# Layer-norm statistics spread by transposing a column of stride 0, and their three sums taken in one group of matmuls

## The chip, the cores and the metric

The kernel runs on one core of one Trainium2 chip. The metric is the time of one execution on the device, in microseconds (us). Times of several executions are given as a median with the lowest and the highest.

## What is computed

A two-layer backbone (a Conformer convolution layer and a bidirectional mLSTM layer, each followed by a squared-ReLU MLP) over 256 context tokens and 256 latent tokens of width 1024. Each of its sub-layers ends in a layer norm of a residual sum. The part that the change touches is the layer norm of layer 0, which runs on both streams:

```python
def layer_norm(x, g, b):
    xf = x.astype(jnp.float32)
    mu = jnp.mean(xf, axis=-1, keepdims=True)
    var = jnp.mean(jnp.square(xf - mu), axis=-1, keepdims=True)
    return ((xf - mu) * lax.rsqrt(var + LN_EPS) * g.astype(jnp.float32) + b.astype(jnp.float32)).astype(x.dtype)
...
        h = layer_norm(ALPHA * h + g1 * y, ln1_g[i], ln1_b[i])
        h = layer_norm(ALPHA * h + g2 * sq_relu_mlp(modulate(h, sh2, sc2), mlp_w1[i], mlp_w2[i]), ln2_g[i], ln2_b[i])
        if need_ctx:
            hc = layer_norm(ALPHA * hc + cg1 * yc, ln1_g[i], ln1_b[i])
            hc = layer_norm(ALPHA * hc + cg2 * sq_relu_mlp(modulate(hc, csh2, csc2), mlp_w1[i], mlp_w2[i]), ...)
```

## The kernel before

In layer 0 the residual stream `x` lies transposed: eight tiles of 128 channels (partitions) by 512 tokens, the context tokens in columns 0 to 255 (`LO`) and the latent tokens in 256 to 511 (`HI`). [...] All large products are done in three single-pass matmuls on a weight split into a high and a low part (`mm3`, lines 180, 183 and 184), each of 256 or 512 columns; ScalarE casts the high part (line 149) and VectorE subtracts it to get the low one (line 150).

The class `Norm` (from line 486) handles one norm of one half, n = 256 tokens, so nb = n/P = 2 blocks of 128 tokens. There are four of them: after the second pointwise convolution (`pw2_epi`, for LO and then HI) and after the first MLP (`feed0`, for HI and then LO). I call them norms A (LO, near 190 to 208 us), B (HI, 218 to 236 us), C (HI, 551 to 567 us) and D (LO, 577 to 597 us). Each goes through these steps:

- `add` (lines 502 and 504) sums the eight tiles on VectorE into `acc`, as they come out of the matmuls.
- `mean` (line 509), after the fourth tile: a matmul with `inv_h` (line 510) gives a provisional mean `k`, the same in every partition, and ScalarE copies it to SBUF (line 511). Then `col` takes the column `kc`, the token-wise value of `k`, from `acc` as it stands.
- `shift` (lines 525 to 531) subtracts `k` from each tile on VectorE, squares the result on ScalarE and adds the squares up in `s2` on VectorE. It is a chain of links, one for each tile.
- `finish` (line 543) takes the columns `mu` (from the complete `acc`) and `ms` (from `s2`), each by `col`; subtracts `kc` from `mu`; forms the variance, its root on ScalarE (line 557), the reciprocal (line 559) and minus mean times reciprocal (line 560). `rn` then has four columns: two of rstd, two of -mean*rstd, with one token in each partition. To use them they must be spread: each token's value has to stand in all 128 partitions, along the free axis. Before the change, VectorE multiplies four copies of the identity by the four columns (`dg`, line 566, a 128x512 tile of four diagonals), and one matmul of `ones` with `dg` (line 571) gives a PSUM bank with rstd in columns 0 to 255 and -mean*rstd in 256 to 511.
- `apply` (lines 577 and 578) multiplies and adds on VectorE, and ScalarE and VectorE turn the result into the next product's input (lines 600 and 601).

`col` (lines 534 to 541) is a group of nb = 2 one-column matmuls, `src` block as the stationary operand and `inv_c` as the moving one (line 538), and one VectorE instruction that scales them into SBUF (line 540). A matmul of two fp32 operands that is not a transpose leaves two records in the trace, each with its own weight load.

The small results lie in PSUM tiles with the tag "ln", of which two can be held at a time; the transposes of the convolution's second half (`silu`, line 975) use the same two while norm A runs. `tmp("L")`, two tiles, holds `dg`, the squares of line 530 and other temporaries.

The order of the instructions on each engine is, with few exceptions (`issue_after`, `keep_in_program_order`), not written out by hand. A planner sets it when the kernel is built: of the instructions whose inputs and tiles are ready by its own estimate of the costs, it takes the one that comes first in the program. So the matmuls of a norm stand in the middle of a run of large matmuls, at the place where the planner took their inputs to be ready. On the chip each engine keeps to that order and waits at a semaphore if the inputs are later.

Line 1808, elsewhere in the kernel, has a stationary operand of stride 0:

```python
nc.tensor.matmul(ps, fold[:, 2 * v + 1:2 * v + 2].broadcast_to([P, P]), ada_n3.sb, start=True, stop=True)
```

Of the kernel before, what the change touches and what calls it, by code (L numbers as in the profile page):

```python
# [8 lines left out]
F32 = mybir.dt.float32  # L9
# [3 lines left out]
ALU = mybir.AluOpType  # L13

P = 128
D = 1024
# [4 lines left out]
T = 512  # L21
# [4 lines left out]
L = 128  # L26
# [44 lines left out]
def hybrid_kernel(ctx: ExitStack, tc: tile.TileContext, xT, vecs_d, wdw_d, ada0_w, ada_w, wg_d, pw1a, pw1, pw2, w1_0, w2_0,  # L71
                  w1_1, w2_1, up_x, up_z, wv, wo, bo_d, wk, wq, wqT, wdown, rows_d, out):
    nc = tc.nc
    PSUM = bass.MemoryType.PSUM
    con = ctx.enter_context(tc.tile_pool(name="con", bufs=1))
# [8 lines left out]
    def nm(s):  # L84
        uid[0] += 1
        return f"{s}_{uid[0]}"
# [3 lines left out]
    def tmp(tag, dt=F32):  # L90
        return tp.tile([P, T], dt, tag=tag, name=nm(tag), bufs={"E": 4, "S": 2, "L": 2, "F": 1}[tag])
# [8 lines left out]
    def psum(tag="mm"):  # L100
        return pp.tile([P, 512], F32, tag=tag, name=nm(tag), bufs={"mm": 3, "ln": 2, "fl": 1, "cv": 2}[tag])
# [23 lines left out]
    ident = con.tile([P, P], F32, name="ident")  # L125
    make_identity(nc, ident)
    ones = con.tile([P, P], F32, name="ones")
# [2 lines left out]
    nc.vector.memset(inv_h, 1.0 / DH)  # L130
    inv_c = con.tile([P, 1], F32, name="inv_c")
    nc.vector.memset(inv_c, 1.0 / D)
    eps = con.tile([P, 1], F32, name="eps")
    nc.vector.memset(eps, EPS)

# [350 lines left out]
    class Norm:  # L486
# [21 lines left out]
        def mean(self):  # L508
            kp = psum("ln")[:, :self.n]
            nc.tensor.matmul(kp, inv_h, self.acc, start=True, stop=True)  # L510
            nc.scalar.copy(self.k, kp)
            self.kc = self.col(self.acc, 2.0 / D)

        def feed(self, t):

# [15 lines left out]
                nc.vector.tensor_tensor(self.s2, self.s2, sq, op=ALU.add)  # L531
            self.i += 1

        def col(self, src, scale):
            nb = self.n // P
            ps = psum("ln")
            for b in range(nb):
                nc.tensor.matmul(ps[:, b:b + 1], src[:, b * P:(b + 1) * P], inv_c, start=True, stop=True)
            c = con.tile([P, nb], F32, name=nm("lc"))
            nc.vector.tensor_scalar(c, ps[:, :nb], scale * D, None, op0=ALU.mult)  # L540
            return c

        def finish(self, fill=()):

            fill = list(fill)
            n, nb = self.n, self.n // P
            if fill:
                fill.pop(0)()
            mu = self.col(self.acc, 1.0 / D)
            if fill:  # L550
                fill.pop(0)()
            ms = self.col(self.s2, 1.0 / D)
            nc.vector.tensor_tensor(mu, mu, self.kc, op=ALU.subtract)
            m2 = con.tile([P, nb], F32, name=nm("lc"))
            nc.vector.tensor_tensor(m2, mu, mu, op=ALU.mult)
            nc.vector.tensor_tensor(ms, ms, m2, op=ALU.subtract)
            nc.scalar.activation(ms, ms, AF.Sqrt, bias=eps)
            rn = con.tile([P, 2 * nb], F32, name=nm("lc"))
            nc.vector.reciprocal(rn[:, :nb], ms)
            nc.vector.scalar_tensor_tensor(rn[:, nb:], mu, -1.0, rn[:, :nb], op0=ALU.mult, op1=ALU.mult)  # L560
            for f_ in fill:
                f_()
            outp = []
            for i in range(0, 2 * nb, 4):
                dg = tmp("L")
                nc.vector.tensor_tensor(
                    dg.rearrange("p (b c) -> p b c", b=4),
                    ident.rearrange("p (o c) -> p o c", o=1).broadcast_to([P, 4, P]),
                    rn[:, i:i + 4].rearrange("p (b o) -> p b o", o=1).broadcast_to([P, 4, P]), op=ALU.mult)
                ps = psum("ln")  # L570
                nc.tensor.matmul(ps, ones, dg, start=True, stop=True)
                outp += [ps[:, j:j + n] for j in range(0, T, n)]
            self.rstd, self.nmr = outp

        def apply(self, f, sl=slice(None)):
            t = self.ts[f][:, sl]
# [1269 lines left out]
    for c in range(4):  # L1846
# [40 lines left out]
        if last:  # L1887
            nc.scalar.activation(con.tile([P, 1], F32, name=nm("warm")), eps, AF.Sqrt)
            for hf in range(2):
                for kt, w in last:  # L1890
                    w2_mm(w, kt, 0, hf)
                residual(0, hf, acc[0][hf], G2)
                if hf == 0:
                    part(acc[1][1], HF[1])
            finish(0)
            for kt, w in last:
                w2_mm(w, kt, 1, 0)
            part(acc[1][0], HF[0])
            for q in range(2):
                quarter(q)  # L1900
            for q, sl in HALVES:
                ps = psum()[:, :C]
                for i, (kt, w) in enumerate(last):
                    mm3t(ps, hid[kt][0][:, BLK[1]], hid[kt][1][:, BLK[1]], w[0][1][:, sl], w[1][1][:, sl],
                         i == 0, i == len(last) - 1)
                quarter(2 + q, ps)
            finish(1)
# [79 lines left out]
```

## Time and profile before

| | |
|---|---|
| time, median of 3 (lowest to highest) | 1675.88 us (1675.58 to 1676.01) |
| time of the profiled execution | 1676.15 us |
| span of the profiled execution | 1674.3 us |
| TensorE busy | 1662.7 us, 99% of the span |
| VectorE busy | 1034.4 us, 62% |
| ScalarE busy | 742.5 us, 44% |
| mean granted TensorE clock | 0.999 |

In the profile PE stands for TensorE's matmuls and PEld for its weight loads, which overlap them; DVE is VectorE, ACT ScalarE, POOL GpSimd, SP SyncE. L571 is line 571 of the kernel. A row of a timeline has the start in us from the span's start, the time taken, the engine, the line, the operation, output and inputs, their shapes, and how many instructions in a row are merged into it. Matmuls overlap: a matmul's own time runs from its issue to its modelled end, so a busy PE isn't told from a fast one by its busy time. What a group of matmuls costs is seen by the starts of the matmuls before and behind it.

### The profile page before, as it was taken

Reading aid. Unit: us, or ns where it says so; the run is one execution under the profiler, and the core shown is the slowest. Engines: PE = TensorE matmul, PEld = TensorE weight load, DVE = VectorE, ACT = ScalarE, POOL = GpSimd, SP = SyncE. Lnnn points to the kernel's source line nnn. Section 1 sums busy time; section 2 is a strip of 40 time slices with the busy share of each in tenths; the row PEclk is TensorE's granted clock in tenths of the full one; section 3 lists DMA queues with packets and bytes.
Section 4 is the critical chain, followed back from the end, with each engine's and each line's share of the span. In section 5 each row is a group of like instructions: output and inputs, shape, how many; then the busy total and the mean of one; then the engine's idle time right before and its main releaser. Section 6 shows DMA issues by size and latency. Waiting matters only on the chain.

```text
span 1674.3 us, 22935 instructions
## 1 busy us (share of the span) xinstructions
PE 1662.7 (99%) x8944; PEld 1369.3 (82%) x8944; DVE 1034.4 (62%) x1877; ACT 742.5 (44%) x1196; POOL 14.3 (1%) x64
## 2 busy tenths in 40 slices
PE   9999999999999999999999999999999999999998
PEld 7665898888888998877788899888878888778887
DVE  6555895666645775752143653464389876786677
ACT  4312573232324466642232542442368654555453
POOL 0000000000000000000000000000000000000001
PEclk9999999999999999999999999999999999999999
DMA  9547223434424065566685753455375555675552
GB/s 356 196 153 273 86 74 114 151 126 144 145 101 151 2 202 191 175 206 248 252 270 170 249 188 120 133 207 168 134 246 187 194 213 212 245 274 188 186 182 95
DMA packets 73035, 301.61 MB, mean 180 GB/s; under 512 B 7422, under 2 KB 23586, under 8 KB 42848
## 3 DMA queue, kind: packets, MB, share of 16 engines
q1 hardware_dynamic: 55216, 285.44, 48.7%
q10 hardware_dynamic: 17712, 14.72, 2.6%
q8 instruction: 70, 1.15, 0.3%
q14 instruction: 37, 0.30, 0.1%
HBM read 284.37 MB, written 15.77 MB: 179 GB/s over the span
## 4 chain that ended last, share of the span: by engine, by line
PE 95%; DVE 2%; DMA 1%; ACT 0%; issue 0%; SPq 0%; DVEq 0%; ACTq 0%
PE mm L180 17%; PE mm L184 17%; PE mm L183 17%; PE mm L195 7%; PE mm L211 4%; PE mm L213 4%; PE mm L196 4%; PE mm L212 4%; PE cv L211 1%; PE cv L213 1%; PE cv L212 1%; PE fl L342 1%; PE ln L180 1%; PE cv L855 1%; PE fl L772 1%; PE ln L183 1%
## 5 line engine op out<-in xcount | busy, mean ns | idle before, releaser
L150 DVE TENSOR_TENSOR wl<-raw,wh 128x1024 fp32r<-128x1024 f32 x344 | 418.6, 1221 | 272.0 <-ACT wh L149 269.6
L149 ACT CAST wh<-raw 128x1024 fp32r<-128x1024 f32 x344 | 358.4, 1050 | 496.2 <-PE mm L183 271.8
L183 PE MATMUL mm<-u,wh 128*128 128x512 f32 (+1 forms) x808 | 291.9, 361 | 0.3 <-DVE u L610 0.2
L180 PE MATMUL mm<-u,wh 128*128 128x512 f32 (+1 forms) x680 | 244.5, 360 | 0.0
L184 PE MATMUL mm<-u,wl 128*128 128x512 f32 (+1 forms) x680 | 241.5, 356 | 0.0
L183 PEld LDWEIGHTS mm<-u,wh 128*128 128x128 f32 x808 | 152.7, 189 | 23.3 <-issue 1.0
L180 PEld LDWEIGHTS mm<-u,wh 128*128 128x128 f32 x680 | 128.5, 189 | 25.8 <-issue 7.2
L184 PEld LDWEIGHTS mm<-u,wl 128*128 128x128 f32 x680 | 128.4, 189 | 18.7 <-issue 1.0
L211 PE MATMUL mm<-wh,xl 128*128 128x512 f32 x256 | 101.1, 395 | 0.8 <-ACT wh L149 0.8
L180 PE MATMUL mm<-xm,wh 128*128 128x512 f32 x256 | 101.0, 395 | 0.0
L212 PE MATMUL mm<-wh,xl 128*128 128x512 f32 x256 | 100.1, 391 | 0.0
L184 PE MATMUL mm<-xm,wl 128*128 128x512 f32 x256 | 99.7, 390 | 0.0
L213 PE MATMUL mm<-wl,xl 128*128 128x512 f32 x256 | 99.4, 392 | 0.3 <-DVE wl L150 0.3
L180 PE MATMUL mm<-hid,wh 128*128 128x512 f32 (+1 forms) x256 | 93.3, 364 | 0.0
L183 PE MATMUL mm<-hid,wh 128*128 128x512 f32 (+1 forms) x256 | 92.8, 363 | 0.0
L184 PE MATMUL mm<-hid,wl 128*128 128x512 f32 (+1 forms) x256 | 92.8, 363 | 0.0
L195 PE MATMUL mm<-x,wh 128*128 128x512 f32 x232 | 81.1, 398 | 0.0
L425 DVE SCALAR_TENSOR_TENSOR S<-ar,cs,S 128x512 f32<-128x512 f32 x56 | 40.8, 750 | 62.0 <-DMA ar<-ada_w 61.6
L183 PE MATMUL mm<-qq,wh 128*128 128x272 f32 x256 | 73.9, 289 | 0.0
L180 PE MATMUL mm<-qq,wh 128*128 128x272 f32 x256 | 73.5, 288 | 0.0
L184 PE MATMUL mm<-qq,wl 128*128 128x272 f32 x256 | 73.5, 288 | 0.0
L195 PE MATMUL mm<-u,wh 128*128 128x512 f32 x192 | 68.7, 398 | 0.0
(533 smaller groups left out, 3269.7 us busy)
## 6 DMA issues: line engine op xcount, KB each, us to landing
raw<-w SPq DMA_DIRECT2D x64, 1024.0 KB, 4.8
raw<-wo SPq DMA_DIRECT2D x32, 1024.0 KB, 4.8
raw<-ada_w SPq DMA_DIRECT2D x24, 1024.0 KB, 6.4
ar<-ada_w SPq DMA_DIRECT2D x80, 256.0 KB, 3.6
raw<-wv SPq DMA_DIRECT2D x16, 1024.0 KB, 7.9
raw<-wqT SPq DMA_DIRECT2D x16, 1024.0 KB, 5.9
raw<-wq SPq DMA_DIRECT2D x16, 1024.0 KB, 5.4
raw<-wk SPq DMA_DIRECT2D x16, 1024.0 KB, 5.6
```

The source lines that it names most:

```text
L149: c = nc.scalar.copy(hi, src)
L150: lastsub[0] = nc.vector.tensor_tensor(lo, src, hi.bitcast(F32), op=ALU.subtract).ins
L180: a = nc.tensor.matmul(ps, wh, xh, start=start, stop=False)
L183: nc.tensor.matmul(ps, wh, xl, start=False, stop=False)
L184: lastmm[0] = nc.tensor.matmul(ps, wl, xh, start=False, stop=stop).ins
L195: todo = [lambda s_, e_: nc.tensor.matmul(ps, wh, r[0], start=s_, stop=e_), lambda s_, e_: nc.tensor.matmul(ps[:, :n], wl, r[0][:, :n], st ...
L196: lambda s_, e_: nc.tensor.matmul(ps[:, :n], wl, r[0][:, :n], start=s_, stop=e_)]
L211: nc.tensor.matmul(ps, xh, wh, start=start, stop=False)
L212: nc.tensor.matmul(ps, xl, wh, start=False, stop=False)
L213: nc.tensor.matmul(ps, xh, wl, start=False, stop=stop)
L342: a = mark_unit[0] = nc.tensor.matmul(ps[32 * j:32 * j + 32], cs[:, kt, 14 - 2 * v:46 - 2 * v], blocks[kt], start=first and kt < 4, stop=l ...
L425: nc.vector.scalar_tensor_tensor(a, w, c, a, op0=ALU.mult, op1=ALU.add)
```

## The change

```diff
+    neg_c = con.tile([P, 1], F32, name="neg_c")
+    nc.gpsimd.memset(neg_c, -1.0 / P)
...
             nc.scalar.copy(self.k, kp)
-            self.kc = self.col(self.acc, 2.0 / D)
...
-        def col(self, src, scale):
-            nb = self.n // P
+        def finish(self):
+
+            n, nb = self.n, self.n // P
             ps = psum("ln")
             for b in range(nb):
-                nc.tensor.matmul(ps[:, b:b + 1], src[:, b * P:(b + 1) * P], inv_c, start=True, stop=True)
-            c = con.tile([P, nb], F32, name=nm("lc"))
-            nc.vector.tensor_scalar(c, ps[:, :nb], scale * D, None, op0=ALU.mult)
-            return c
-
-        def finish(self, fill=()):
-
-            fill = list(fill)
-            n, nb = self.n, self.n // P
...
-            mu = self.col(self.acc, 1.0 / D)
...
-            ms = self.col(self.s2, 1.0 / D)
-            nc.vector.tensor_tensor(mu, mu, self.kc, op=ALU.subtract)
+                nc.tensor.matmul(ps[:, nb + b:nb + b + 1], self.s2[:, b * P:(b + 1) * P], inv_c, start=True, stop=True)
+            for b in range(nb):
+                sl = slice(b * P, (b + 1) * P)
+                nc.tensor.matmul(ps[:, b:b + 1], self.acc[:, sl], inv_c, start=True, stop=False)
+                nc.tensor.matmul(ps[:, b:b + 1], self.k[:, sl], neg_c, start=False, stop=True)
+            mv = con.tile([P, 2 * nb], F32, name=nm("lc"))
+            nc.vector.tensor_copy(mv, ps[:, :2 * nb])
+            mu, ms = mv[:, :nb], mv[:, nb:]
...
-            outp = []
-            for i in range(0, 2 * nb, 4):
-                dg = tmp("L")
-                nc.vector.tensor_tensor(
-                    dg.rearrange("p (b c) -> p b c", b=4),
-                    ident.rearrange("p (o c) -> p o c", o=1).broadcast_to([P, 4, P]),
-                    rn[:, i:i + 4].rearrange("p (b o) -> p b o", o=1).broadcast_to([P, 4, P]), op=ALU.mult)
-                ps = psum("ln")
-                nc.tensor.matmul(ps, ones, dg, start=True, stop=True)
-                outp += [ps[:, j:j + n] for j in range(0, T, n)]
-            self.rstd, self.nmr = outp
+            ps = psum("ln")
+            for j in range(2 * nb):
+                nc.tensor.transpose(ps[:, j * P:(j + 1) * P], rn[:, j:j + 1].broadcast_to([P, P]), ident)
+            self.rstd, self.nmr = ps[:, :n], ps[:, n:2 * n]
```

Two things are changed in each of the four norms. The three column sums, which stood in three places (`kc` in `mean`, `mu` and `ms` in `finish`), are taken in one place, with `ms` first; instead of `kc`, the sum over the partitions of `k` times -1/128 is accumulated onto the sum of `acc`, and one VectorE copy takes all four columns out of PSUM. And the spread is done by four transposes of 128x128: each reads one column of `rn` as if it were a 128x128 block with all its columns equal (a free stride of 0), so that its transpose has that column along the free axis in every partition. `neg_c` is a new 128x1 constant, set by GpSimd. `fill`, which no caller gave, is gone.

More of the change, by code (lines that the diff above doesn't have):

```diff
@@ L532, in shift @@
             self.i += 1
-        def col(self, src, scale):
-            nb = self.n // P
+        def finish(self):
+            n, nb = self.n, self.n // P
             ps = psum("ln")
             for b in range(nb):
-                nc.tensor.matmul(ps[:, b:b + 1], src[:, b * P:(b + 1) * P], inv_c, start=True, stop=True)
-            c = con.tile([P, nb], F32, name=nm("lc"))
-            nc.vector.tensor_scalar(c, ps[:, :nb], scale * D, None, op0=ALU.mult)
-            return c
-        def finish(self, fill=()):
-            fill = list(fill)
-            n, nb = self.n, self.n // P
-            if fill:
-                fill.pop(0)()
-            mu = self.col(self.acc, 1.0 / D)
-            if fill:
-                fill.pop(0)()
-            ms = self.col(self.s2, 1.0 / D)
-            nc.vector.tensor_tensor(mu, mu, self.kc, op=ALU.subtract)
+                nc.tensor.matmul(ps[:, nb + b:nb + b + 1], self.s2[:, b * P:(b + 1) * P], inv_c, start=True, stop=True)
[6 more added lines that the diff above has]
+            mu, ms = mv[:, :nb], mv[:, nb:]
             m2 = con.tile([P, nb], F32, name=nm("lc"))
@@ L560, in finish @@
             nc.vector.scalar_tensor_tensor(rn[:, nb:], mu, -1.0, rn[:, :nb], op0=ALU.mult, op1=ALU.mult)
-            for f_ in fill:
-                f_()
-            outp = []
-            for i in range(0, 2 * nb, 4):
-                dg = tmp("L")
-                nc.vector.tensor_tensor(
-                    dg.rearrange("p (b c) -> p b c", b=4),
-                    ident.rearrange("p (o c) -> p o c", o=1).broadcast_to([P, 4, P]),
-                    rn[:, i:i + 4].rearrange("p (b o) -> p b o", o=1).broadcast_to([P, 4, P]), op=ALU.mult)
-                ps = psum("ln")
-                nc.tensor.matmul(ps, ones, dg, start=True, stop=True)
-                outp += [ps[:, j:j + n] for j in range(0, T, n)]
-            self.rstd, self.nmr = outp
+            ps = psum("ln")
+            for j in range(2 * nb):
+                nc.tensor.transpose(ps[:, j * P:(j + 1) * P], rn[:, j:j + 1].broadcast_to([P, P]), ident)
+            self.rstd, self.nmr = ps[:, :n], ps[:, n:2 * n]
         def apply(self, f, sl=slice(None)):
```

## The prediction

> **What bounds the kernel now.** I read the page first, then the stretches of the span with the norms in them, then the lines and tiles of `Norm`, and last TensorE's timeline around its matmuls.
>
> ```profile
> PE 1662.7 (99%) x8944; PEld 1369.3 (82%) x8944; DVE 1034.4 (62%) x1877; ACT 742.5 (44%) x1196; POOL 14.3 (1%) x64
> PE 95%; DVE 2%; DMA 1%; ACT 0%; issue 0%; SPq 0%; DVEq 0%; ACTq 0%
> ```
>
> ```profile
> 183.30:240.00 56.70, 56.52 (x458) 54.90 (x457) 49.59 (x146) 35.67 (x75) 0.00 (x0) 1.00 0.22 82
> 545.00:615.00 70.00, 69.97 (x568) 68.33 (x567) 53.96 (x138) 35.70 (x66) 0.79 (x9) 1.00 0.23 78
> ```
>
> TensorE is the bound: 95% of the chain that ended last. In the two stretches with the norms (length, then busy time of PE, PEld, DVE, ACT and POOL, granted clock, DMA share, GB/s) it idles 0.18 us of 56.70 and 0.03 us of 70.00, at a clock of 1.00. VectorE has 7 and 16 us to spare. So only two things here can move the end: how long TensorE's stream is held up by the norms' own matmuls, and whether a new wait opens in it. What VectorE saves is worth nothing by itself.
>
> Who waits for whom in the norms is in the rows by line and tile (count, shortest/median/longest in ns, first and last start; under them the idle time before them, or who waited for them):
>
> ```profile
> L538 PE MATMUL ln<-inv_c,ln x48: 164/250/271, 189.2 to 593.3; 128*128 128x1 f32 x48
>   issue: 0.4, 2
>   ACT S L978: 0.2, 1
>   DVE lc L540: 6.0, 9
> ...
> L540 DVE TENSOR_SCALAR lc<-ln x12: 147/159/160, 189.8 to 593.5; 128x2 f32<-128x2 f32 x12
> L553 DVE TENSOR_TENSOR lc<-lc,lc x4: 148/152/160, 201.1 to 592.3; 128x2 f32<-128x2 f32 x4
> L566 DVE TENSOR_TENSOR L<-ident,lc x4: 692/692/693, 205.9 to 594.7; 128x512 f32<-128x512 f32 x4
> ...
> L571 PE MATMUL ln<-L,ones x8: 591/592/668, 206.8 to 596.0; 128*128 128x512 f32 x8
>   PE mm L180: 0.3, 1
>   PE mm L184: 0.2, 1
>   issue: 0.2, 1
> ```
>
> TensorE stood idle before three of the twelve one-column groups (0.4 + 0.2 = 0.6 us) and before three of the four spreads (0.3 + 0.2 + 0.2 = 0.7 us); VectorE waited 6.0 us for the sums. TensorE as a rule comes to a norm's matmuls after their inputs, not before.
>
> **What a group costs TensorE.** Matmuls overlap, so I take starts: from the last large matmul before a group to the second one behind it, less two usual steps.
>
> ```profile
> 201.84 0.28 PE L184 MATMUL mm<-u,wl 128*128 128x256 f32 x1
> 201.96 0.28 PE L180 MATMUL mm<-u,wh 128*128 128x256 f32 x1
> 202.08 0.50 PE L538 MATMUL ln<-inv_c,ln 128*128 128x1 f32 x4
> 202.44 0.36 PE L183 MATMUL mm<-u,wh 128*128 128x256 f32 x1
> 202.65 0.28 PE L184 MATMUL mm<-u,wl 128*128 128x256 f32 x1
> ...
> 183.31 0.28 PE L184 MATMUL cv<-u,wl 128*128 128x256 f32 x1
> 183.43 0.96 PE L350 MATMUL fl<-fold,F 128*128 128x12 f32 x8
> 184.24 0.36 PE L180 MATMUL mm<-u,hid 128*128 128x256 f32 x1
> 184.44 0.28 PE L183 MATMUL mm<-u,hid 128*128 128x256 f32 x1
> ...
> 234.77 0.28 PE L184 MATMUL mm<-u,wl 128*128 128x256 f32 x1
> 234.88 1.02 PE L571 MATMUL ln<-L,ones 128*128 128x512 f32 x2
> 235.34 0.68 PE L180 MATMUL mm<-u,wh 128*128 128x256 f32 x1
> 235.86 0.28 PE L183 MATMUL mm<-u,wh 128*128 128x256 f32 x1
> ...
> 190.00 0.28 PE L183 MATMUL mm<-u,hid 128*128 128x256 f32 x1
> 190.11 0.60 PE L975 MATMUL ln<-ident,u 128*128 128x128 f32 x4
> 190.47 0.37 PE L184 MATMUL mm<-u,hid 128*128 128x256 f32 x1
> 190.68 0.28 PE L180 MATMUL mm<-u,hid 128*128 128x256 f32 x1
> ```
>
> The usual step of a 256-column matmul is 201.96 - 201.84 = 0.12 us. A sum of two one-column matmuls (four records) that nothing held up costs 202.65 - 201.96 - 0.24 = 0.45 us. Eight records of 12 columns cost 184.44 - 183.31 - 0.24 = 0.89 us. A spread that nothing held up (norm B) costs 235.86 - 234.77 - 0.24 = 0.85 us. Four transposes of 128x128 cost 190.68 - 190.00 - 0.24 = 0.44 us.
>
> **The change, part by part.**
>
> The three sums. Before, three groups of four records: 3 x 0.45 = 1.35 us a norm. After, one group of six matmuls, twelve records: from 0.45 at four and 0.89 at eight, 0.11 us a record, 0.89 + 0.44 = 1.33 us. The group saves nothing in itself; at best, if all twelve go at 0.09 us (from 202.08 to 202.44 are four) with one change-over of 0.08 us, it costs 1.16 us, 0.19 less. I take 0.02 a norm, 0.1 us in all, and keep 0.8 us as the good end.
>
> The spread. A matmul of two long fp32 records gives way to four transposes: 0.85 - 0.44 = 0.41 us a norm, 1.64 us in four. That is the main term. The trace before has no transpose of a stride-0 block, but it has a stationary operand of stride 0 (line 1808), whose weight load (its median 190 ns) is as long as an ordinary one (mean 189 ns):
>
> ```profile
> L180 PEld LDWEIGHTS mm<-u,wh 128*128 128x128 f32 x680 | 128.5, 189 | 25.8 <-issue 7.2
> ...
> L1808 PEld LDWEIGHTS mm<-F,fold x4: 188/190/190, 1553.7 to 1554.8; 128*128 128x128 f32 x4
> L975 PE MATMUL ln<-ident,u x32: 270/272/328, 162.2 to 195.8; 128*128 128x128 f32 x32
> ```
>
> So I take 0.44 us for the four. Bounds: at the dear end the transposes don't overlap, each 0.272 us from the row of L975, 1.09 us in all, 0.24 more than the spread of before; at the cheap end a one-column record's 0.09 us each, 0.36 us, which adds 0.3 us over four norms to the gain.
>
> The Trainium skill bears on the dear end: "TensorE: Matmul & The Clock Gate", Part 4 (PE-mode transpose), gives some 275 ns for a 128x128 transpose within a kernel and says that the full clock doesn't engage for this mode. The 272 ns of L975 agrees as a length. But the rows at 190.11 and 190.47 show four in 0.36 us from start to start, and the clock over this stretch, with those transposes in it, was 1.00. By the rule read as a cost per transpose, the spread would lose 0.24 us a norm and the sum below would turn to +1 us; by the rows it gains 0.41.
>
> The waits. Of the 0.6 us before sums, the 0.2 us behind L978 was `kc` waiting for one of the two "ln" tiles; that group is gone from there, and per norm the tag is taken twice after `mean` in place of three times, besides the one for `kc`. The other 0.4 us were groups placed a little early, and the new group has as much cause for that: it now waits for `s2`, the last of the three inputs. The 0.7 us before the spreads were the wait for `dg`; the transposes wait for `rn` instead, one VectorE instruction earlier, and the planner brings them forward by as much as it thinks `dg` took. I expect most of it again. So 1.3 us of waits become about 1.1: 0.2 us saved. Bounds: all 1.3 us go, or each of eight groups waits 0.3 us, the longest seen: 2.4 us, 1.1 more.
>
> Off the path. VectorE loses three scalings of 0.16 us, one subtraction of 0.15 and `dg` of 0.69 a norm, and gains one copy of about 0.16 (as L540): 1.2 us less a norm. It is hidden behind TensorE either way: no norm's `apply` makes TensorE wait. On the latency from the last `s2` to the spread the change is neutral: the sum group is 1.33 - 0.45 = 0.9 us longer and one small subtraction and product come behind it, and 0.69 us of `dg` and 0.41 us of the spread go. If that cover were gone, a few tenths of a us a norm would show. `neg_c`, one 128x1 set on GpSimd at the start, is needed 180 us later; GpSimd is 1% busy. No DMA is issued or moved by the change itself, so no queue is passed.
>
> The sum: -0.1 - 1.64 - 0.2 = -1.9 us. The profiled execution took 1676.15 us, 1.85 more than its span, and would take 1674.2. It was 0.27 us over the median of the runs, 1675.88, so I forecast a median of 1674.0 us.
>
> **The rivals.**
>
> All good ends: the sum group at 1.16 us (0.8 in all), the transposes at 0.36 (1.64 + 0.3), no wait left (1.3): -4.0 us, 1671.9. For it: VectorE is freer and the "ln" tiles less contended. Against: none of the waits was for VectorE's load, and eight records did cost twice four.
>
> The new wait, which ends slower. The sum group sits in TensorE's queue as one block of 1.3 us behind `s2`; the large matmuls behind it can't pass it. The links of `s2` go back and forth between two engines:
>
> ```profile
> L530 ACT ACTIVATE L<-x x28: 405/418/424, 192.0 to 590.9; 128x256 f32<-128x256 f32 x28
> L531 DVE TENSOR_TENSOR ln<-ln,L x28: 412/418/426, 192.6 to 592.0; 128x256 f32<-128x256 f32 x28
> ```
>
> One link is 0.42 + 0.42 = 0.84 us. If the planner puts the group two links early in each norm, TensorE waits 1.7 us four times, 6.7 us: 1674.0 + 6.7 = 1680.7. It decides the sign from 1.9/4 = 0.5 us a norm. For it: weight casts on ScalarE and VectorE go between the links, and the order around them may come out otherwise. Against: the `ms` groups waited for the same `s2` before and TensorE idled under 0.3 us at any of them.
>
> Serial transposes: 4 x 0.24 lost in place of 1.64 won, with the other terms: 1675.88 + 0.96 - 0.3 = 1676.5. For it: a stride-0 read in a transpose isn't in the trace. Against: the rows of L975.
>
> **How the numbers follow.** What a measurement of this kernel can tell from no change is about 0.2%, 3.4 us: faster means under 1672.5, slower over 1679.2. Chances: the forecast 0.52, all good ends 0.22, the new wait 0.16, serial transposes 0.10. A changed order further on, which a planner's small shifts can bring, widens each by some 1.5 us. Faster by over 0.2%: 0.18 of the second case and 0.08 of the first, 0.26. Slower: most of the third and a little of the fourth, 0.16. Within 0.2%: 0.58. The range, 1671.2 to 1679.0, takes in nearly all of the first and fourth cases, two thirds of the second and a part of the third.
>
> **What would show it.** Right: one group of twelve L538-like records a norm, about 1.3 us by the starts around it, four transposes at about 0.44 us in place of 0.85, VectorE busy some 5 us less, and the same clock. Wrong on the spread: transposes whose starts lie 0.27 us apart. Wrong on the sums: TensorE idle before the group, put down to VectorE's L531. Wrong as a whole: a difference that lies outside the four norms, in weight casts or in another order of the large matmuls.

## The result, and the profile after

| | before | after |
|---|---|---|
| time, median of 10 runs each, measured together (lowest to highest) | 1675.97 us (1675.58 to 1676.80) | 1679.61 us (1678.08 to 1681.73) |
| time of the profiled execution | 1676.15 us | 1679.66 us |
| span | 1674.3 us | 1677.7 us |
| VectorE busy | 1034.4 us | 1032.0 us |

The ratio of after to before is 1.002, with a 95% interval of 1.0012 to 1.0028. The kernel became 3.6 us slower, where 1.9 us less had been forecast.

The profile after: the busy times of the page; the three stretches (the second reaches 8 us further than before), columns as before; the waits of TensorE (total us, times, longest); and TensorE's timeline around the matmuls of norm B. The three lines of the large matmuls are now L182, L185 and L186; the sums are L540, L543 and L544, the transposes L557.

```profile
PE 1662.1 (99%) x8952; PEld 1369.8 (82%) x8952; DVE 1032.0 (62%) x1861; ACT 742.1 (44%) x1196; POOL 14.4 (1%) x65
```

```profile
183.30:240.00 56.70, 55.82 (x461) 54.95 (x460) 48.74 (x141) 36.66 (x77) 0.00 (x0) 1.00 0.23 80
183.30:248.00 64.70, 61.46 (x495) 60.38 (x494) 56.12 (x161) 42.03 (x89) 0.00 (x0) 0.97 0.20 71
545.00:615.00 70.00, 69.97 (x581) 69.44 (x580) 52.10 (x131) 33.16 (x62) 0.79 (x9) 1.00 0.24 84
```

```profile
PE mm L182 <- ACT E L1036: 3.0, 2, 2.4
```

```profile
228.83 0.28 PE L185 MATMUL mm<-u,wh 128*128 128x256 f32 x1
228.95 0.50 PE L540 MATMUL ln<-inv_c,ln 128*128 128x1 f32 x4
229.31 0.36 PE L543 MATMUL ln<-inv_c,ln 128*128 128x1 f32 x2
...
230.21 0.36 PE L186 MATMUL mm<-u,wl 128*128 128x256 f32 x1
230.41 0.28 PE L182 MATMUL mm<-u,wh 128*128 128x256 f32 x1
...
232.80 0.28 PE L186 MATMUL mm<-u,wl 128*128 128x256 f32 x1
232.92 0.60 PE L557 MATMUL ln<-ident,lc 128*128 128x128 f32 x4
233.27 0.36 PE L182 MATMUL mm<-u,wh 128*128 128x256 f32 x1
233.47 0.29 PE L185 MATMUL mm<-u,wh 128*128 128x256 f32 x1
```

In norm B the group of sums costs 230.41 - 228.83 - 0.24 = 1.34 us and the four transposes 233.47 - 232.80 - 0.24 = 0.43 us. Read in the same way, the groups of sums of norms A, C and D cost 1.69, 1.63 and 1.52 us, and their transposes 0.66, 0.46 and 0.53. All together that is 6.18 + 2.08 = 8.26 us. Before, the same reading gives 6.16 us for the sums and 4.27 us for the spreads, 10.43 together. So the norms' own matmuls did become 2.2 us cheaper, all of it in the spread.

The loss lies just behind norm B. In the second stretch TensorE is busy for 61.46 of 64.70 us, against 64.52 before, and the mean granted clock is 0.97 against 1.00:

```profile
183.30:248.00 64.70, 64.52 (x525) 62.90 (x524) 57.57 (x168) 43.27 (x91) 0.00 (x0) 1.00 0.20 72
```

TensorE waits twice for L1036 (L1051 before), 3.0 us in all, a wait that the profile of before does not have. This is the first instruction behind a product of the first MLP, in its function `e1`:

```python
r, q = tmp("E")[:, :ps.shape[-1]], tmp("E")[:, :ps.shape[-1]]
nc.scalar.activation(r, ps, AF.Relu)
nc.vector.tensor_tensor(q, r, r, op=ALU.mult)
```

Its `ps` is one of three PSUM tiles with the tag "mm". While norm B ends, TensorE already works on the MLP's products for the LO half; the Relu empties their tile, and the products behind take that tile next. ScalarE's timeline after, then before, has these Relus (L1036, L1051) among norm B's sixteen affines (L585, L600), which `affine_half` issues behind each `apply`:

```profile
231.92 0.30 ACT L551 ACTIVATE lc<-lc,eps 128x2 f32<-128x2 f32 x1 [2.62 <-DVE lc L550]
233.91 0.38 ACT L1036 ACTIVATE E<-mm 128x256 f32<-128x256 f32 x1 [1.70 <-PE mm L186]
234.46 0.60 ACT L585 ACTIVATE u<-x,cb,ca 128x256 fp32r<-128x256 f32 x1 [0.16 <-DVE x L563]
234.97 0.59 ACT L585 ACTIVATE S<-x,cb,ca 128x256 f32<-128x256 f32 x1
...
237.74 0.36 ACT L1036 ACTIVATE E<-mm 128x256 f32<-128x256 f32 x1
238.00 0.59 ACT L585 ACTIVATE u<-x,cb,ca 128x256 fp32r<-128x256 f32 x1
...
242.44 0.59 ACT L585 ACTIVATE S<-x,cb,ca 128x256 f32<-128x256 f32 x1
242.93 0.39 ACT L151 CAST hid<-E 128x256 fp32r<-128x256 f32 x1
243.22 0.65 ACT L1036 ACTIVATE E<-mm 128x256 f32<-128x256 f32 x2
```

```profile
232.79 0.29 ACT L557 ACTIVATE lc<-lc,eps 128x2 f32<-128x2 f32 x1 [1.06 <-DVE lc L556]
233.99 0.74 ACT L1051 ACTIVATE E<-mm 128x256 f32<-128x256 f32 x2 [0.91 <-PE mm L184]
...
235.18 0.38 ACT L1051 ACTIVATE E<-mm 128x256 f32<-128x256 f32 x1
...
237.10 0.60 ACT L600 ACTIVATE u<-x,cb,ca 128x256 fp32r<-128x256 f32 x1 [0.59 <-DVE x L578]
```

Before, three Relus ran at 233.99 to 235.18, and the first affine at 237.10. After, the first affine runs at 234.46; the second Relu stands behind six of them and runs at 237.74, and the third behind all sixteen, at 243.22. An affine takes 234.97 - 234.46 = 0.5 us of the queue. TensorE's timeline shows what that costs:

```profile
237.20 0.28 PE L186 MATMUL mm<-u,wl 128*128 128x256 f32 x1
238.15 0.39 PE L182 MATMUL mm<-u,u 128*128 128x256 f32 x1 [0.68 <-ACT E L1036]
238.38 0.28 PE L185 MATMUL mm<-u,u 128*128 128x256 f32 x1
...
241.01 0.28 PE L186 MATMUL mm<-u,u 128*128 128x256 f32 x1
243.65 0.58 PE L182 MATMUL mm<-u,u 128*128 128x256 f32 x1 [2.36 <-ACT E L1036]
244.03 0.41 PE L185 MATMUL mm<-u,u 128*128 128x256 f32 x1
244.25 0.41 PE L186 MATMUL mm<-u,u 128*128 128x256 f32 x1
...
246.59 0.30 PE L185 MATMUL mm<-u,u 128*128 128x256 f32 x1
246.73 0.28 PE L186 MATMUL mm<-u,u 128*128 128x256 f32 x1
```

```profile
243.65:246.60 2.95, 2.95 (x14) 2.95 (x15) 2.95 (x10) 1.72 (x5) 0.00 (x0) 0.50 0.02 6
```

The first wait costs 238.38 - 237.20 - 0.24 = 0.94 us and the second 244.03 - 241.01 - 0.24 = 2.78 us. Behind the second, matmuls start 0.21 us apart in place of 0.12, at a granted clock of 0.50 (the stretch in the last fence): from 244.03 to 246.59 twelve steps take 2.56 us in place of 1.44, another 1.1 us. Together the loss is 4.8 us. The two traces matched instruction by instruction give the ledger: the large matmuls run 0.9 us earlier than before behind norm B, 3.9 us later behind these waits, 2.8 us later behind norm D, and 3.3 us later near the end, with the last 0.5 us of that at a pause near 1650 us that comes and goes in other kernels (below). The profiled executions are 3.5 us apart.

### The profile page after: what moved, and what is told of

The parts are those of the page before. It is cut to its first block, busy times and chain, and to the rows that moved or that the text cites. A ratio compares the mean times of both kernels' runs of the same rounds, so it can differ in the third digit from the quotient of the medians.

```text
span 1677.7 us, 22930 instructions
## 1 busy us (share of the span) xinstructions
PE 1662.1 (99%) x8952; PEld 1369.8 (82%) x8952; DVE 1032.0 (62%) x1861; ACT 742.1 (44%) x1196; POOL 14.4 (1%) x65
## 4 chain that ended last, share of the span: by engine, by line
PE 94%; DVE 3%; ACT 1%; DMA 1%; issue 1%; SPq 0%; DVEq 0%; ACTq 0%
PE mm L182 17%; PE mm L185 17%; PE mm L186 17%; PE mm L197 7%; PE mm L213 4%; PE mm L215 4%; PE mm L214 4%; PE mm L198 3%; PE cv L213 1%; PE fl L344 1%; PE cv L215 1%; PE cv L214 1%; DVE wl L152 1%; PE ln L182 1%; PE cv L840 1%; PE fl L757 1%
## 5 line engine op out<-in xcount | busy, mean ns | idle before, releaser
L185 PE MATMUL mm<-u,wh 128*128 128x512 f32 (+1 forms) x808 | 291.6, 361 | 0.3 <-DVE u L595 0.2
L182 PE MATMUL mm<-u,wh 128*128 128x512 f32 (+1 forms) x680 | 244.0, 359 | 0.0
L186 PE MATMUL mm<-u,wl 128*128 128x512 f32 (+1 forms) x680 | 241.2, 355 | 0.0
L185 PEld LDWEIGHTS mm<-u,wh 128*128 128x128 f32 x808 | 152.6, 189 | 22.6 <-DVE u L595 0.5
L182 PEld LDWEIGHTS mm<-u,wh 128*128 128x128 f32 x680 | 128.5, 189 | 25.2 <-issue 6.7
L186 PEld LDWEIGHTS mm<-u,wl 128*128 128x128 f32 x680 | 128.4, 189 | 18.6 <-issue 0.8
L182 PE MATMUL mm<-xm,wh 128*128 128x512 f32 x256 | 101.0, 395 | 0.0
L186 PE MATMUL mm<-xm,wl 128*128 128x512 f32 x256 | 99.7, 390 | 0.0
L182 PE MATMUL mm<-hid,wh 128*128 128x512 f32 (+1 forms) x256 | 93.3, 364 | 0.0
L186 PE MATMUL mm<-hid,wl 128*128 128x512 f32 (+1 forms) x256 | 92.8, 363 | 0.0
L185 PE MATMUL mm<-hid,wh 128*128 128x512 f32 (+1 forms) x256 | 92.8, 363 | 0.0
L185 PE MATMUL mm<-qq,wh 128*128 128x272 f32 x256 | 73.9, 289 | 0.0
L182 PE MATMUL mm<-qq,wh 128*128 128x272 f32 x256 | 73.5, 288 | 0.0
L186 PE MATMUL mm<-qq,wl 128*128 128x272 f32 x256 | 73.5, 288 | 0.0
```

The lines of the kernel that those rows point to most:

```text
L182: a = nc.tensor.matmul(ps, wh, xh, start=start, stop=False)
L185: nc.tensor.matmul(ps, wh, xl, start=False, stop=False)
L186: lastmm[0] = nc.tensor.matmul(ps, wl, xh, start=False, stop=stop).ins
```

## The experiments

All times are medians; the kernel before, run on the same chip between them, had 1676.05 us (28 runs) beside the first four and 1676.06 us (33 runs) beside the last four. The theories, as the expectations name them: Q, that norm B's affines come ahead of the Relus in ScalarE's queue; T, that the transposes themselves cost the time; S, that the three sums in one group do; C, that a chance stretch of half clock explains a time; O, that holding the affines back is a gain of its own. Only two of the eight intervals below leave 1 out (the order alone, and by little the whole change with the affines behind the Relus), and two end at it. Differences of 1 to 2 us are therefore read from the traces, with the times beside them.

**The transposes alone**, on the kernel before:

```diff
-            outp = []
-            for i in range(0, 2 * nb, 4):
...
+            ps = psum("ln")
+            for j in range(2 * nb):
+                nc.tensor.transpose(ps[:, j * P:(j + 1) * P], rn[:, j:j + 1].broadcast_to([P, P]), ident)
+            self.rstd, self.nmr = ps[:, :n], ps[:, n:2 * n]
```

> Before, with the spread of all four norms by transposes; the three sums stay in three groups. In the order that the planner gives it, the second of the three Relus of the first MLP stands ahead of norm B's 16 affine instructions on ScalarE, the third behind 14 of them. Theory Q (ScalarE's queue: norm B's affines come earlier and keep the Relus from freeing PSUM): TensorE waits once, some 2 to 3.5 us near 240 us, with a slower clock behind it; the spreads save 1.6 to 2 us; 1677 to 1679 us. Rival T (the transposes of a stride-0 column cost TensorE more than the rows around them show, or lower its clock): no long wait at 240 us, 1679 to 1680 us.

Measured: 1677.81 us (1675.95 to 1678.49, 11 runs), ratio 1.0007 with an interval of 0.9998 to 1.0016. The waits and TensorE's timeline of this kernel:

```profile
PE mm L180 <- ACT E L1044: 2.2, 1, 2.2
```

```profile
239.82 0.28 PE L184 MATMUL mm<-u,u 128*128 128x256 f32 x1
242.29 0.39 PE L180 MATMUL mm<-u,u 128*128 128x256 f32 x1 [2.19 <-ACT E L1044]
242.52 0.28 PE L183 MATMUL mm<-u,u 128*128 128x256 f32 x1
```

The wait for the Relu comes with the transposes alone, once instead of twice; here the second Relu stays ahead of the affines, and only the third falls behind them. The wait just about eats what the spreads save. Theory T had no long wait and 1679 to 1680 us; the median lies in Q's range. In the profiled execution (1677.18 us) the matmuls behind the wait go on at 0.12 us. The runs fall in two groups: five, with a mean granted clock of 0.999, at 1675.95 to 1677.18, and six, with 0.998, at 1677.81 to 1678.49. That would fit a half clock behind this wait in about every second execution, but only one execution was profiled.

**The sums alone**, that is the whole change with the old spread:

```diff
-            for j in range(2 * nb):
-                nc.tensor.transpose(ps[:, j * P:(j + 1) * P], rn[:, j:j + 1].broadcast_to([P, P]), ident)
...
+                nc.tensor.matmul(ps, ones, dg, start=True, stop=True)
```

> The change without its transposes: sums in one group, the spread by the identity times the column and a matmul with ones, as before. All three Relus stand ahead of the affines on ScalarE. Theory Q: no wait behind a Relu; the sums in one group save 0 to 0.6 us; 1675.4 to 1676.0 us. Rival T: 1675.4 to 1676.0 us as well. Rival S (the one group of sums is what costs, by holding TensorE behind s2): 1678 to 1680 us.

Measured: 1677.44 us (1676.63 to 1679.36, 11 runs), ratio 1.0007, interval 0.9998 to 1.0016. No wait for a Relu is in the profile. None of the theories had this time: Q and T were 1.4 us too low, S 0.6 us too high. The profiled execution was the longest of the eleven (1679.36 us); in it the granted clock is 0.50 from 61.73 to 65.14 us, far ahead of the norms, and from there comes theory C. The kernel was measured again, below.

**The order alone**, on the kernel before, with its arithmetic untouched: the second Relu of the LO half is placed behind six of norm B's affines and the third behind all sixteen, as in the kernel after.

```diff
+                behind = {1: 16 + 5, 2: 16 + 15}.get(m) if keep and c == 0 and s == 0 else None
+                with tc.issue_after(half_ins[behind]) if behind else nullcontext():
-                nc.scalar.activation(r, ps, AF.Relu)
+                    nc.scalar.activation(r, ps, AF.Relu)
```

> Before, with nothing of the change; only the order on ScalarE is made that of the changed kernel: the second Relu of the first MLP behind 6 affines of norm B, the third behind all 16. Theory Q: TensorE waits for the Relus near 238 and 244 us and its clock falls behind the longer wait; 3 to 5 us over before, more than the change since nothing is saved: 1679 to 1681 us. Rivals T and S: within 1 us of before, 1675.5 to 1677 us.

Measured: 1680.94 us (1680.55 to 1682.48, 6 runs), ratio 1.003, interval 1.0018 to 1.0041: 4.9 us more than before, with neither the transposes nor the new sums. Its waits, the row of the first, and the stretch behind the second and longer one:

```profile
PE mm L180 <- ACT E L1055: 4.2, 2, 2.4
```

```profile
239.73 0.39 PE L180 MATMUL mm<-u,u 128*128 128x256 f32 x1 [1.82 <-ACT E L1055]
```

```profile
245.23:248.60 3.37, 3.37 (x16) 3.37 (x17) 3.37 (x11) 1.71 (x5) 0.00 (x0) 0.51 0.02 5
```

Two waits and the half clock are there. So the place of two Relus in ScalarE's queue is enough for a loss of this size. It is no exact copy: the affines of before start later, and the first wait is 1.82 us in place of 0.68.

**The whole change with the affines behind the Relus.** Norm B's `apply` and affines are issued from the third Relu on:

```diff
+        if s == 1:
+            held.append(lambda: ln1_apply(s, sl))
+        else:
+            ln1_apply(s, sl)
...
-                nc.scalar.activation(r, ps, AF.Relu)
+                third = nc.scalar.activation(r, ps, AF.Relu).ins
+                if held and m == 2:
+                    with tc.issue_after(third):
+                        held.pop()()
```

> The whole change, with norm B's affines on ScalarE queued behind the third Relu of the first MLP (no computation differs). Theory Q: the waits of 3.0 us and the slower clock behind them go and the saving at the norms' own matmuls stays: 1673.3 to 1674.5 us, faster than before. Rivals T and S: 1678.5 to 1680 us, as the change. If part of the loss lies further on in another order: between the two, about 1676.

Measured: 1674.61 us (1673.89 to 1675.42, 11 runs), ratio 0.999, interval 0.9981 to 0.9999; 0.1 us above Q's range. The wait is gone, and so is the low clock:

```profile
183.30:248.00 64.70, 64.50 (x535) 63.82 (x534) 57.00 (x162) 44.21 (x94) 0.00 (x0) 1.00 0.20 69
```

The two halves add up: 1674.61 - 1676.05 = -1.4 us for the change without the wait, and +4.9 us for the wait without the change, make +3.5; the change itself had +3.6. That the sum comes so close is partly luck: by the matched traces the loss behind norm B is 6.2 us in the kernel with the order alone (profiled at 1682.12 us) and 4.8 us in the change.

**The old spread in norm B only**, the rest as after:

```diff
+            if self.old:
...
+                    nc.tensor.matmul(ps, ones, dg, start=True, stop=True)
...
+        lnp[s].old = s == 1
```

> The whole change, but norm B alone keeps the diagonal and the product with ones. Theory Q (the spread of norm B ends 2 us sooner, its affines stand before two Relus on ScalarE, and TensorE waits for the PSUM tiles): norm B's apply falls back, the three Relus stand ahead of the affines, no wait of TensorE for the Relu's line over 0.5 us, and the time is 1675.9 less what three norms still save (about 0.5 us each): 1674 to 1675. Theory T (the new operations themselves cost the time): three of four norms keep them, so three quarters of the loss stay, 1678 to 1679.

Measured: 1675.62 us (1675.07 to 1676.93, 11 runs), ratio 0.9997, interval 0.9989 to 1.0006. T is out: three of the four transposed spreads run here, and all of the loss is gone. There is no wait for a Relu. The time is 0.6 us above the range that Q gave. By the matched traces the large matmuls do run 1.5 us earlier than before behind norm D, as Q had it for three norms; 0.4 us of that is lost near 1425 us and 0.4 us near 1650. Of the next two rows the first is from TensorE's timeline before, the second from that of this kernel:

```profile
1425.42 0.50 PE L211 MATMUL mm<-wh,xl 128*128 128x512 f32 x1 [0.75 <-ACT wh L149]
```

```profile
1424.14 0.50 PE L213 MATMUL mm<-wh,xl 128*128 128x512 f32 x1 [1.13 <-ACT wh L151]
```

A wait for a weight's cast, 830 us behind the last of the four norms, is 0.4 us longer. What makes it so was not found.

**The transposes alone with the affines behind the Relus**, the first experiment with the edit of the fourth.

> The kernel before with the transposes alone, and norm B's apply held behind the third Relu of the first MLP. Theory Q: the wait of 2.2 us that the transposes alone had is gone, and four spreads at 0.4 us less stand: 1674.0 to 1674.8, about the same as the whole change with that order (1674.6). Theory S (putting the three sums in one group costs some 1 us by itself, as its run alone hinted with 1677.4): 1 us below the whole change with that order, 1673.3 to 1673.8.

Measured: 1674.16 us (1673.73 to 1675.80, 11 runs), ratio 0.9991, interval 0.9982 to 1.0000. This is the lowest median of all, 1.9 us below before, where the spread alone had been put at 1.64 us. A gain of the sums in one group is not seen: with them the same order takes 1674.61 us, 0.45 us more, which is less than either interval can tell. S, which wanted 1 us between the two, is not borne out in that size either.

**The order on the kernel before**, nothing else:

> The kernel before with nothing but the order: norm B's apply held behind the third Relu. Before, the three Relus stood ahead of the affines already, so theory Q expects no change: 1675.5 to 1676.3. If holding the affines back is a gain of its own, apart from the change (theory O), the time is 1674.5 or less, and the gain of the other ordered kernels is not the transposes'.

Measured: 1676.41 us (1675.39 to 1677.68, 11 runs), ratio 1.0002, interval 0.9993 to 1.0010; 0.1 us above Q's range. No gain of the order by itself is seen, and O, which wanted 1674.5 or less, is out. Its profile has a wait that before's has not:

```profile
PE ln L212 <- DVE hid L150: 0.4, 1, 0.4
```

Around it the matmuls pause behind the one at 1648.55 us; in after they pause behind the one at 1651.92, at the same place of the program. A few tenths of a us come and go there between kernels that are the same in that place.

**The sums alone, again.**

> The three sums in one group alone, a second time, for its time of 1677.4 us that neither theory had named, and for another profile. If the sums in one group cost a time of their own (theory S), it is 1677 to 1678 again, and the profile shows it in the four norms, 0.3 us or more at each. If the first run met executions with a stretch of half clock near 61 us that has nothing to do with the norms (theory C), it is 1675.9 to 1676.6, and the profile shows the norms within 0.2 us of before.

Measured: 1677.46 us (1676.85 to 1678.20, 11 runs), ratio 1.0009, interval 1.0000 to 1.0018. The time is the same as in the first run, so C falls as its explanation. But S said that the norms would show it, and they don't:

```profile
183.30:248.00 64.70, 64.41 (x522) 62.62 (x521) 56.70 (x161) 42.51 (x91) 0.00 (x0) 1.00 0.20 71
...
545.00:615.00 70.00, 69.97 (x567) 68.33 (x566) 53.01 (x132) 36.05 (x66) 0.79 (x9) 1.00 0.23 78
```

```profile
1425.96 0.50 PE L213 MATMUL mm<-wh,xl 128*128 128x512 f32 x1 [1.02 <-ACT wh L151]
```

TensorE idles in these stretches 0.1 us more than before, at the full clock. Matched with the trace of before, its large matmuls run 0.25 us later behind norm D; 0.3 us come at the cast near 1425 us (1.02 in place of 0.75) and 0.35 at the end near 1650. That accounts for 0.9 of the 1.05 us between the two profiled executions. Why the old spread with the new sums has these late waits, and the transposes with the new sums have them less, stays open; it is an effect of 0.1% far from the change.

## Why the prediction was wrong

- **The transposes**: right. 0.44 us was forecast, the undisturbed ones took 0.43 and 0.46. "Serial transposes" falls: four start within 0.35 us (232.92 to 233.27), 0.09 us each, with a column of stride 0 as well as with an ordinary block.
- **The three sums**: right. 1.33 us forecast for a group, 1.34 measured in norm B; over four norms 6.16 us before and 6.18 after.
- **The waits**: about right. Sums and spreads with their waits were to save 1.9 us; they saved 2.2 by the starts around the groups (1.9 by the matched traces: 0.85 in A and B, 1.09 in C and D), and the two kernels with the affines held back were 1.4 and 1.9 us faster than before; in their traces the large matmuls gain 1.9 us on before from norm A to behind norm D, in both.
- **VectorE**: 1.2 us less a norm was forecast, 4.8 in all; the page shows 2.4. The operations themselves lost about what was forecast: 2.77 us of `dg`, 1.89 of scalings and 0.62 of subtractions are gone, and 0.64 of copies are new, 4.6 us in the sum of their times. Records of neighbouring instructions overlap in time (before, VectorE's records add up to 1133.5 us) and the page counts such time once (1034.4 us), so its busy time falls by less.
- **The step that failed** is the one "Off the path": the freed time of VectorE is "hidden behind TensorE either way: no norm's `apply` makes TensorE wait", and "the change is neutral" on the latency to the spread. Both halves were wrong. In norm B the spread starts at 232.92 in place of 234.88 us: the root on ScalarE comes 0.9 us sooner (231.92 for 232.79), and from there to the spread it takes 1.0 us in place of 2.1, for `dg` is gone. Then the transposes end 0.4 us sooner. An `apply` that comes early makes nobody wait for it; but its sixteen affines go to ScalarE, and there the planner, which takes what is ready, put them ahead of the Relus that free the PSUM tiles. The prediction asked who waits for `apply`, and not what stands behind its successors in a queue and who waits for that. The price left out was 4.8 us by the starts (4.9 us with the order alone), two and a half times the whole gain.
- **The rivals**: "The new wait" had the right sign and nearly the right time (1680.7 for 1679.6), but by luck, for it had another place: the sums wait no longer for `s2` than before (0.2 us in the group's row below). Its place in the list of what would show it was the last one, a difference outside the four norms. One figure of the prediction doesn't agree with its own sum: with 0.24 us lost at each spread the sum is +0.7 us, which gives the rival's 1676.5, and not +1.

```profile
L540 PEld LDWEIGHTS ln<-inv_c,ln 128*128 128x128 f32 x16 | 2.1, 190 | 0.6 <-issue 0.3 <-DVE ln L532 0.2
```

The range ended at 1679.0, 0.6 us short, since it priced waits of the norms alone and gave a changed order further on some 1.5 us.

## What to carry to other kernels

Where an engine's order is made from what is ready first, making one result earlier can put its followers ahead of something more urgent in an in-order queue. For each step that comes earlier, read the queue of the engine that consumes it in the timeline: what stands within a few instructions behind, and does it release a tile for the engine that is the bound? Here the gain at the norms' own matmuls stands in the traces (1.9 us), and a fixed order got it back: 1674.2 us for the transposes alone with the affines held behind the third Relu, 1676.1 before, 1679.6 as the change stood. The first of these differences is at the edge of what the runs can tell; the second is not.

## What the runs showed of the hardware

A pause of TensorE can cost more than its length. In after, 2.64 us from start to start (a wait of 2.36) are followed by a granted clock of 0.50; the trace's record of it lasts 3.413 us and adds 1.1 us. In the kernel with only the order changed, a wait of the same length is followed by the same. In the kernel with the transposes alone, 2.47 us from start to start (a wait of 2.19) left the clock at 1.00 in the profiled execution.

The trace's record of the clock suggests what makes the difference. In all ten traces each stretch at one clock that ends within the work lasts a whole multiple of 3.413 us: in after 238.933 us (70 times), then the low 3.413, then 1426.771 (418 times); in before 1665.704 (488 times). So the clock changed only at the edges of windows of 3.413 us, and these lie differently in each execution (the first edge seen is at 4.25 us in after, at 5.92 in before). In after a window runs from 239.77 to 243.18 us; TensorE idles 3.41 - 1.52 = 1.89 us of it, and the clock falls at its end, 0.47 us before the matmuls go on. In the kernel with the transposes alone the same count from its first edge puts one at 241.16 us, in the middle of the wait, with 1.06 us of idle time in the window ahead of it and 1.13 us in the one behind, and the clock stays (after, then the transposes alone; columns as before):

```profile
239.77:243.18 3.41, 1.52 (x13) 1.32 (x11) 3.41 (x11) 3.41 (x8) 0.00 (x0) 1.00 0.00 0
243.18:246.59 3.41, 2.94 (x13) 2.94 (x14) 3.41 (x11) 2.19 (x7) 0.00 (x0) 0.50 0.02 5
```

```profile
237.75:241.16 3.41, 2.35 (x20) 2.15 (x18) 3.41 (x12) 3.41 (x8) 0.00 (x0) 1.00 0.00 0
241.16:244.57 3.41, 2.28 (x19) 2.28 (x20) 3.41 (x11) 3.39 (x10) 0.00 (x0) 1.00 0.02 5
```

By this reading it matters how a wait falls on the windows, and not its length alone. It would fit that the times of one kernel fall in groups: of the ten runs of the change, seven have a mean granted clock of 0.998 and 1679.56 to 1681.73 us, and three have 0.999 and 1678.08 to 1678.97. No experiment moved a wait against the windows, so this stays a reading. Nor is idle time all that counts: in the first run of the sums alone the clock fell at 61.73 us, behind a window with only 0.17 us of idle time.

The Trainium skill ("TensorE: Matmul & The Clock Gate", Part 1, "What's actually happening") has the clock halve after an idle window of about 3.4 us that runs free of the program. The 3.413 us of the traces agrees with the length of that window, and the edges that differ between executions agree with its running free; but the window ahead of the low clock was idle for 1.89 of its 3.41 us only, which is less than the page has it.
